# Where the first gate rows come from, where one modulation row is made, and where the last norms keep their tiles

## The chip, the cores and the metric

The kernel is one program on one core of a Trainium2 chip. Its time is the device time of one execution in microseconds (us). The profile is of one execution; its span runs from the first to the last instruction of the core. Engines are called PE (matmul), PEld (weight load), DVE, ACT, POOL and SP as in the profile; SP and POOL also issue DMAs, each on its own queue, in order.

## The reference, cut to what matters

One layer of a hybrid backbone on 512 latent tokens (and 256 context tokens) of width 1024. A token mixer (two families of gated scans, output projection, layer norm) comes first. The part that matters here is the second sublayer, a product-key expert retrieval over 128 x 128 single-neuron experts:

```python
q = (t @ w_query)...                      # 8 heads, two halves
s1, s2 = scores of the halves against 128 first keys and 128 second keys
v1, i1 = top_k(s1, 16); v2, i2 = top_k(s2, 16)
top_s, pos = top_k(all pair sums, 16)     # 16 experts per head, 128 per token
idx = first key * 128 + second key
g = softmax(top_s)
act = gelu(einsum('thkd,td->thk', expert_u[idx], t))
y   = einsum('thk,thkd->td', g * act, expert_v[idx])
x   = layer_norm(alpha * x + g2 * y) * gamma + beta      # the output
```

`g2` is one of six modulation rows, silu(c) times 1024 columns of `w_ada` plus a bias, the same for all tokens.

## The kernel before, in words

**Dense and fetched tokens.** Tokens are in four blocks of 128. For three blocks (`ND` = 3, `TD` = 384 tokens) the experts are computed densely: all 16,384 rows of `u` and `v` go through PE, and a gate matrix G[expert, token], zero where a token did not choose the expert, multiplies the activations. The fourth block (and the dot products with `u` of the last 16 tokens of the third) is fetched: POOL gathers, for one choice k at a time, one row of `u` or `v` for each of 128 tokens into a ring of six tiles `erow` (512 KB each, `fetched`, L1202 to L1249), and DVE multiplies and accumulates it (`dots` at L1235, `yg` at L1248).

**The gate matrix.** `gate_block` (L1115) makes it for 8 tokens at a time from one-hot matrices: DVE builds them, PE multiplies them into `pG`, ACT copies that to `stage`, a tile [128 second keys, 128 first keys, 32 tokens]. Each of the 12 stage tiles (2 MB) is stored to the DRAM tensor `Gd`. `gated` (L1165) reads it back, eight first keys and all 384 tokens at a time (`Gn`, 1.5 MB, two buffers), 16 times.

**Chunks.** There are 64 chunks of two first keys (256 experts). `hidden` (L1141) loads a chunk of `u` (`ur`, 1 MB), splits it into a high and a low part in `load_split` (`uh` by ACT at L1136, `ul` by DVE at L1137), makes 2 x 24 matmuls into `pH` and applies the activation into a `gel` tile. Part of `hidden` runs while the gate matrix is built (28 chunks are spilled to DRAM, `Hd`, and come back later); the rest runs in the main part, one beside each output chunk. An output chunk is `rows` (load `vr`, 1 MB, and split into `vh`, `vl`), `gated` (copy of 16 tokens' gates by ACT at L1177, product of `gel` and `Gn` by DVE at L1181, split into `ah` by ACT at L1186 and `al` by DVE at L1187) and `combine`: 2 x 18 matmuls `y` that accumulate in six PSUM banks over all chunks. The chunks' order is 0 to 3, 32 to 63, 4 to 31, and chunks 0 to 3 need the first eight first keys. The crossing is the place where the gate stage ends and the first `y` matmuls start. `vh` and `vl` have two buffers, one for each half of a chunk.

**The order of work.** A scheduler lays out each engine's instructions once, from the program and a cost model; an engine then runs them strictly in that order and waits at each for what it needs. POOL is in the program's order from the fourth block's picks on, ACT in the last three chunks.

**`g2`'s rows.** `mods_last` (L251) is a generator. After the last `hidden`, each further chunk advances it by one step: load 512 KB of `w_g2`, and multiply and sum what the step before loaded (L259). After eight steps `m2[:, 24:32]` holds the sums, and the bias is added (L264). `to_rows` (L266) turns that into rows: one PE transpose, one ACT copy (L272), one store to DRAM on POOL's queue (L273). `mod_row` (L275) loads the row as a broadcast on POOL's queue. Before, `to_rows` is called in the tail, just ahead of `mod_row`.

**The tail.** The last three chunks (`TAIL` = 3) are prepared, then multiplied block by block and half by half, so that `finish` (L1251), the residual sum and the layer norm of a block, can run while PE works on later blocks. `finish(3)`, the fetched block's, comes first and needs no PE; then `finish(0)`, `finish(1)`, `finish(2)`. `finish` has two tiles of 4 KB a partition, `x1` (loaded at L1256) and `r`; before, both are halves of a `vr` buffer of the later `v` ring. The row tiles g2, gamma and beta lie in a `Gn` buffer.

Of the kernel before, what the change touches and what calls it, by code (L numbers as in the profile page):

```python
# [8 lines left out]
F32 = mybir.dt.float32  # L9
F32R = mybir.dt.float32r  # L10
# [4 lines left out]
AF = mybir.ActivationFunctionType  # L15
# [4 lines left out]
D = 1024  # L20
# [11 lines left out]
class Net:  # L32
# [218 lines left out]
    def mods_last(self, pool):  # L251

        nc, a = self.nc, self.a
        sr = pool.tile([128, D], F32, name="silr")
        nc.sync.dma_start(sr, self.sild.to_broadcast([128, D]))
        m2 = self.m2[:, 24:32]
        for j in range(9):
            if j:
                nc.vector.scalar_tensor_tensor(w, w, 1.0, sr, op0=OP.mult, op1=OP.mult, accum_out=m2[:, j - 1:j])  # L259
            if j < 8:  # L260
                w = pool.tile([128, D], F32, name="wg2")
                nc.sync.dma_start(w, a["w_g2"][j])
                yield
        nc.vector.tensor_tensor(m2, m2, self.b2[:, 24:32], op=OP.add)  # L264

# [668 lines left out]
class Peer:  # L934
# [10 lines left out]
    GT = 32  # L945
# [169 lines left out]
    def gate_block(self, w, ps, b, kg):  # L1115

        nc, GT, GB = self.nc, self.GT, self.GB
        for q in range(128 // GT):
            stage = w.tile([128, 128, GT], F32, name="stage", bufs=2)
            for i in range(GT // GB):  # L1120
                self.gate_group(w, ps, kg, q * GT + i * GB, stage[:, :, i * GB:(i + 1) * GB])
                if i == GT // GB - 1:
                    nc.sync.dma_start(self.Gd[b * (128 // GT) + q], stage)
                yield
# [40 lines left out]
    def gated(self, n, pool, vpool, bufs, mark=None, home=None):  # L1165
# [4 lines left out]
        if 2 * n % self.GN == 0:  # L1170
            self.Gn = pool.tile([128, NG, self.GN, self.GT], F32, name="Gn", bufs=2)
            nc.sync.dma_start(self.Gn, self.Gd[:, :, 2 * n:2 * n + self.GN, :].rearrange("g m n t -> m g n t"))
# [9 lines left out]
        if home:  # L1182
            ah, al = (t.rearrange("p a b -> p (a b)")[:, 0:2 * self.TD].rearrange("p (e t) -> p e t", e=2) for t in home)
        else:
            ah, al = (vpool.tile([128, 2, self.TD], F32R, name=f"a{i}", bufs=bufs) for i in "hl")
# [65 lines left out]
    def finish(self, b, y, w, ring, rows, out):  # L1251
        nc = self.nc
        g2, gam, bet = rows
        two = ring.tile([128, 2, 8, 128], F32, name="vr", bufs=2)
        x1, r = (two[:, i].rearrange("p k c -> p (k c)") for i in range(2))
# [12 lines left out]
    def run(self, es, out):  # L1268
# [18 lines left out]
        with ExitStack() as e0:  # L1287
            gl = e0.enter_context(tc.tile_pool(name="gel", bufs=1, side="right", reuse_waits="tile"))
            up_es = e0.enter_context(ExitStack())
# [93 lines left out]
            with ExitStack() as e1:  # L1383
                w = e1.enter_context(tc.tile_pool(name="main", bufs=1, reuse_waits="tile"))
                yp = e1.enter_context(tc.tile_pool(name="yps", bufs=1, space=PSUM, reuse_waits="tile"))
# [5 lines left out]
                for i, m in enumerate(seq[:64 - self.TAIL]):  # L1391
# [12 lines left out]
                    elif i > first + 1:  # L1404
                        next(g2, None)
# [4 lines left out]
                    ops = self.gated(m, w, w, self.TAIL - 1, mark), v  # L1410
# [4 lines left out]
                for _ in g2:  # L1415
                    pass
# [4 lines left out]
                for c, m in enumerate(tail):  # L1421
# [6 lines left out]
                    acts.append(self.gated(m, w, w, self.TAIL - 1, mark, home and home[2]))  # L1428

                rows = w.tile([128, NG, self.GN, self.GT], F32, name="Gn", bufs=2)  # L1430
                rows = rows.rearrange("p g n t -> p (g n t)").rearrange("p (i d) -> p i d", i=3)
                n.to_rows(slice(24, 32), w, hps, "pH", n.q0[1][:, 0:128])
# [6 lines left out]
                self.finish(3, (yg[:, :512], yg[:, 512:]), bits, vp, rows, out)  # L1439
                for b in range(ND):  # L1440
# [4 lines left out]
                    self.finish(b, self.y[b], bits, vp, rows, out)  # L1445
# [32 lines left out]
```

## Time and profile before

| | |
|---|---|
| time before | 1745.32 us median of 3 runs (1743.29 to 1746.83) |
| the profiled execution | 1744.65 us, of which the span is 1742.7 us and 1.95 us lie around it |
| busy, share of the span | PE 95%, PEld 83%, DVE 83%, ACT 48%, POOL 28% |
| granted TensorE clock | 0.984 of full speed on average |
| DMA | 439.15 MB, 252 GB/s over the span |

A busy PE is modelled, so 95% is not PE at its peak. An engine's idle time counts only where it is what the end waits for; the view of the engines by stretches, the engines' timelines and the chain that ended last tell where that is. A timeline row gives the start, the busy time, the engine, the line, the operation with its output and inputs, how many instructions were merged into the row, and in brackets how long the engine sat idle before it and what ended that.

### The profile page before, as it was taken

The page shows a single profiled execution, that of the slowest core. Times are in us where ns is not written, and L with a number is a line of the kernel's source. Part 1 is how long each engine was busy: PE and PEld are TensorE (multiplying, and loading weights), DVE is VectorE, ACT ScalarE, POOL GpSimd, SP SyncE. Part 2 cuts the span into 40 slices and gives each one's busy share as a digit, 9 for nine tenths or more (in the row PEclk, how much of TensorE's full clock was granted, in tenths as well). Part 3 has the DMA queues.
Part 4 walks back from the last instruction along what each step waited for, and adds up shares of the span by engine and source line. Part 5 has one row for each costly group of instructions (what it writes and reads, how often), then busy time and mean ns, then how long its engine had stood idle before and what let it go on. Part 6 is the DMA issues. An engine that isn't in the chain of part 4 may idle for free. (4 is left out here: it accounts for less than half of the span.)

```text
span 1742.7 us, 27586 instructions
## 1 busy us (share of the span) xinstructions
PE 1657.3 (95%) x10440; PEld 1450.2 (83%) x10440; DVE 1455.1 (83%) x2888; ACT 833.2 (48%) x1413; POOL 486.9 (28%) x323
## 2 busy tenths in 40 slices
PE   6999999989999999999996999999999999999995
PEld 3888877877788999999996899999999998778884
DVE  6689888877989999999995887787787777778777
ACT  4667677655233364777663333333333333233331
POOL 0000000000043002232573554454555453234300
PEclk9999999989999999999998999999999999999998
DMA  9345345134322247889889989989989989999962
GB/s 330 117 146 164 129 145 179 58 144 153 145 87 72 98 156 273 296 331 339 327 320 399 357 307 340 348 303 339 350 306 342 341 287 368 364 321 354 340 210 97
DMA packets 128999, 439.15 MB, mean 252 GB/s; under 512 B 12465, under 2 KB 44625, under 8 KB 109922
## 3 DMA queue, kind: packets, MB, share of 16 engines
q1 hardware_dynamic: 88018, 289.94, 47.1%
q0 software_dynamic: 40272, 145.36, 22.9%
q8 instruction: 81, 1.33, 0.3%
q10 hardware_dynamic: 576, 2.10, 0.3%
q14 instruction: 52, 0.43, 0.1%
HBM read 388.95 MB, written 48.40 MB: 251 GB/s over the span
## 5 line engine op out<-in xcount | busy, mean ns | idle before, releaser
L141 PE MATMUL pH<-hh,ul 128*128 128x368 f32 x1024 | 339.0, 332 | 4.1 <-DVE ul L1137 4.1
L139 PE MATMUL pH<-hh,uh 128*128 128x368 f32 x1024 | 339.4, 331 | 1.8 <-ACT gels L1155 1.8
L140 PE MATMUL pH<-hl,uh 128*128 128x368 f32 x1024 | 337.0, 329 | 0.0
L139 PE MATMUL y<-vh,ah 128*128 128x512 f32 x756 | 297.2, 393 | 16.6 <-ACT ah L1186 16.5
L140 PE MATMUL y<-vl,ah 128*128 128x512 f32 x756 | 296.5, 392 | 2.3 <-DVE vl L1137 2.3
L141 PE MATMUL y<-vh,al 128*128 128x512 f32 x756 | 295.6, 392 | 1.4 <-DVE al L1187 1.4
L1219 POOL DMA_INDIRECT erow<-in_v_dram,ix x128 | 214.0, 1672 | 268.6 <-DVE yg L1248 142.4
L1219 POOL DMA_INDIRECT erow<-in_u_dram,ix x128 | 206.8, 1616 | 228.5 <-DVE erow L1235 127.1
L1137 DVE TENSOR_TENSOR vl<-vr,vh 128x1024 fp32r<-128x1024 f32 x126 | 153.7, 1222 | 111.6 <-ACT vh L1136 111.4
L1136 ACT ACTIVATE uh<-ur 128x1024 fp32r<-128x1024 f32 x128 | 135.6, 1060 | 218.7 <-PE pH L140 197.3
L1136 ACT ACTIVATE vh<-vr 128x1024 fp32r<-128x1024 f32 x126 | 131.9, 1055 | 169.0 <-PE y L141 134.0
L141 PEld LDWEIGHTS pH<-hh,ul 128*128 128x128 f32 x1024 | 192.0, 188 | 5.8 <-DVE ul L1137 5.8
L139 PEld LDWEIGHTS pH<-hh,uh 128*128 128x128 f32 x1024 | 192.3, 188 | 3.5 <-ACT gels L1155 2.3
L140 PEld LDWEIGHTS pH<-hl,uh 128*128 128x128 f32 x1024 | 192.2, 188 | 1.2
L139 PEld LDWEIGHTS y<-vh,ah 128*128 128x128 f32 x756 | 143.1, 189 | 47.6 <-ACT ah L1186 18.9
L141 PEld LDWEIGHTS y<-vh,al 128*128 128x128 f32 x756 | 143.1, 189 | 32.8 <-DVE al L1187 2.7
L140 PEld LDWEIGHTS y<-vl,ah 128*128 128x128 f32 x756 | 143.2, 189 | 31.3 <-DVE vl L1137 2.7
L1235 DVE SCALAR_TENSOR_TENSOR erow<-erow,h 128x1024 f32<-128x1024 f32 x128 | 151.8, 1220 | 15.7 <-DMA erow<-in_u_dram,ix 15.7
L1248 DVE SCALAR_TENSOR_TENSOR yg<-erow,q,yg 128x1024 f32<-128x1024 f32 x127 | 162.9, 1283 | 0.1
L1137 DVE TENSOR_TENSOR ul<-ur,uh 128x1024 fp32r<-128x1024 f32 x128 | 154.8, 1220 | 9.7 <-ACT uh L1136 9.6
L139 PE MATMUL pc<-hTh,wh 128*128 128x512 f32 (+1 forms) x304 | 109.6, 361 | 0.3 <-ACT G L381 0.3
L140 PE MATMUL pc<-hTl,wh 128*128 128x512 f32 (+1 forms) x304 | 108.1, 356 | 0.0
(408 smaller groups left out, 3045.0 us busy)
## 6 DMA issues: line engine op xcount, KB each, us to landing
ur<-in_uT_dram SPq DMA_DIRECT2D x64, 1024.0 KB, 7.8
vr<-in_vd_dram SPq DMA_DIRECT2D x64, 1024.0 KB, 6.7
Gd<-stage SPq DMA_DIRECT2D x12, 2048.0 KB, 10.0
Gn<-Gd SPq DMA_DIRECT2D x16, 1536.0 KB, 13.0
wraw<-in_w_cf_dram SPq DMA_DIRECT2D x24, 512.0 KB, 4.0
wada<-in_w_ada_dram SPq DMA_DIRECT2D x48, 256.0 KB, 3.0
Hd<-gels SPq DMA_DIRECT2D x28, 368.0 KB, 5.2
gel<-Hd SPq DMA_DIRECT2D x28, 368.0 KB, 6.0
```

The lines of the kernel that those rows point to most:

```text
L139: mm(out, lh, rh, start=start, stop=False)
L140: mm(out, lh, rl, start=False, stop=False)
L141: mm(out, ll, rh, start=False, stop=stop)
L1136: nc.scalar.activation(hi, raw[:, e], AF.Copy)
L1137: self.mark = nc.vector.tensor_tensor(lo, raw[:, e], hi, op=OP.subtract).ins
L1219: nc.gpsimd.indirect_dma_start(out=e, out_offset=None, in_=a["v" if src == "v" else "u"], in_offset=bass.IndirectOffsetOnAxis(ap=ix[:, j:j ...
L1235: nc.vector.scalar_tensor_tensor(e, e, 1.0, h2, op0=OP.mult, op1=OP.mult, accum_out=dots[:, j:j + 1])
L1248: nc.vector.scalar_tensor_tensor(y, e, act[:, j:j + 1], y, op0=OP.mult, op1=OP.add)
```

## The change

1. **First gates on chip.** When a stage tile is full, ACT copies its first eight first keys into a `Gn` tile that stays on chip (12 copies of 128 x 256), and the store to `Gd` leaves these keys out (1.875 MB in place of 2 MB). `gated` doesn't load `Gn` for chunk 0. The two `Gn` buffers now come from two pools, one opened ahead of the `u` ring and one in the main part, and `new_gates` takes them in turn. `gated` takes its `ah` and `al` tiles ahead of the load.
2. **`g2`'s rows in the main part.** `mods_last` yields True after the bias is added, and the main loop then calls `to_rows`. The tail only calls `mod_row`.
3. **Last norms in the fetched rows' ring.** `finish` takes `x1` and `r` as two tiles of the `erow` ring.

```diff
@@ -260,8 +260,9 @@
             if j < 8:
                 w = pool.tile([128, D], F32, name="wg2")
                 nc.sync.dma_start(w, a["w_g2"][j])
-                yield
+                yield False
         nc.vector.tensor_tensor(m2, m2, self.b2[:, 24:32], op=OP.add)
+        yield True
 
     def to_rows(self, js, pool, ps, tag, row=None):
 
@@ -1120,7 +1121,9 @@
             for i in range(GT // GB):
                 self.gate_group(w, ps, kg, q * GT + i * GB, stage[:, :, i * GB:(i + 1) * GB])
                 if i == GT // GB - 1:
-                    nc.sync.dma_start(self.Gd[b * (128 // GT) + q], stage)
+                    at = b * (128 // GT) + q
+                    nc.scalar.activation(self.Gn[:, at], stage[:, 0:self.GN, :], AF.Copy)
+                    nc.sync.dma_start(self.Gd[at, :, self.GN:, :], stage[:, self.GN:, :])
                 yield
 
 
@@ -1162,13 +1165,23 @@
             r = self.gel[n] = ring.tile([128, 2, self.TD], F32, name="gel", bufs=self.AHEAD + 1)
             self.nc.sync.dma_start(r[:, :, :self.TU], self.Hd[n - self.AHEAD])
 
-    def gated(self, n, pool, vpool, bufs, mark=None, home=None):
+    def new_gates(self):
+
+        self.gates.append(self.gates.pop(0))
+        self.Gn = self.gates[-1].tile([128, self.TD // self.GT, self.GN, self.GT], F32, name="Gn")
+        return self.Gn
+
+    def gated(self, n, vpool, bufs, mark=None, home=None):
 
         nc = self.nc
         NG, NU = self.TD // self.GT, self.TU // self.GT
         rest = self.TU % self.GT
-        if 2 * n % self.GN == 0:
-            self.Gn = pool.tile([128, NG, self.GN, self.GT], F32, name="Gn", bufs=2)
+        if home:
+            ah, al = (t.rearrange("p a b -> p (a b)")[:, 0:2 * self.TD].rearrange("p (e t) -> p e t", e=2) for t in home)
+        else:
+            ah, al = (vpool.tile([128, 2, self.TD], F32R, name=f"a{i}", bufs=bufs) for i in "hl")
+        if 2 * n % self.GN == 0 and n:
+            self.new_gates()
             nc.sync.dma_start(self.Gn, self.Gd[:, :, 2 * n:2 * n + self.GN, :].rearrange("g m n t -> m g n t"))
         g = self.gel.pop(n)
         g4 = g.rearrange("p n (g t) -> p n g t", t=self.GT)
@@ -1179,10 +1192,6 @@
             for t in [(slice(0, NU),)] + [(NU, slice(0, rest))] * (rest > 0):
                 at = (slice(None), slice(None), *t)
                 nc.vector.tensor_tensor(g4[at], g4[at], gates[at], op=OP.mult)
-        if home:
-            ah, al = (t.rearrange("p a b -> p (a b)")[:, 0:2 * self.TD].rearrange("p (e t) -> p e t", e=2) for t in home)
-        else:
-            ah, al = (vpool.tile([128, 2, self.TD], F32R, name=f"a{i}", bufs=bufs) for i in "hl")
         nc.scalar.activation(ah, g, AF.Copy)
         nc.vector.tensor_tensor(al, g, ah, op=OP.subtract)
         return ah, al
@@ -1251,8 +1260,7 @@
     def finish(self, b, y, w, ring, rows, out):
         nc = self.nc
         g2, gam, bet = rows
-        two = ring.tile([128, 2, 8, 128], F32, name="vr", bufs=2)
-        x1, r = (two[:, i].rearrange("p k c -> p (k c)") for i in range(2))
+        x1, r = (ring.tile([128, D], F32, name="erow", bufs=self.LOOK + 1) for _ in range(2))
         nc.sync.dma_start(x1, self.n.x1d[b])
         halves = [slice(hf * 512, (hf + 1) * 512) for hf in range(2)]
         st = w.tile([128, 12], F32, name="stz").rearrange("p (h s) -> p h s", h=2)
@@ -1286,6 +1294,8 @@
         yg = n.yg
         with ExitStack() as e0:
             gl = e0.enter_context(tc.tile_pool(name="gel", bufs=1, side="right", reuse_waits="tile"))
+            self.gates = [e0.enter_context(tc.tile_pool(name="gates", bufs=1, side="right", reuse_waits="tile"))]
+            self.new_gates()
             up_es = e0.enter_context(ExitStack())
             up = up_es.enter_context(tc.tile_pool(name="uring", bufs=1, side="right", reuse_waits="tile"))
             nh, asked = 0, 0.0
@@ -1382,6 +1392,7 @@
                             more(first + (out_to - first) * at / groups - asked)
             with ExitStack() as e1:
                 w = e1.enter_context(tc.tile_pool(name="main", bufs=1, reuse_waits="tile"))
+                self.gates.insert(0, w)
                 yp = e1.enter_context(tc.tile_pool(name="yps", bufs=1, space=PSUM, reuse_waits="tile"))
                 self.y = [tuple(yp.tile([128, 512], F32, name=f"y{b}{hf}") for hf in range(2)) for b in range(ND)]
                 ahead = self.AHEAD - 1
@@ -1402,18 +1413,17 @@
                             first = i
                             g2 = n.mods_last(vp)
                     elif i > first + 1:
-                        next(g2, None)
+                        if next(g2, False):
+                            n.to_rows(slice(24, 32), w, hps, "pH", n.q0[1][:, 0:128])
                     fetch(rate)
                     v = self.rows(m, vp if vp and i > first + 1 and (i - first) % 2 == 0 else w)
                     if nh == 64 and i + ahead < 64:
                         self.back(seq[i + ahead], gl)
-                    ops = self.gated(m, w, w, self.TAIL - 1, mark), v
+                    ops = self.gated(m, w, self.TAIL - 1, mark), v
                     for e in range(2):
                         for b in range(ND):
                             self.combine(2 * m, e, b, ops)
                 fetch(256)
-                for _ in g2:
-                    pass
                 manual.close()
                 e1.enter_context(tc.manual_schedule(engines={mybir.EngineType.Activation}))
                 tail = seq[64 - self.TAIL:]
@@ -1425,24 +1435,23 @@
                         [t[:, 2 * j:2 * j + 2, :].rearrange("p a (b c) -> p (a b) c", c=128) for t in (self.hh, self.hl)]
                         for j in range(3)]
                     vs.append(self.rows(m, (vp, w)[(64 - self.TAIL + c - first) % 2], home and home[:2]))
-                    acts.append(self.gated(m, w, w, self.TAIL - 1, mark, home and home[2]))
-
-                rows = w.tile([128, NG, self.GN, self.GT], F32, name="Gn", bufs=2)
+                    acts.append(self.gated(m, w, self.TAIL - 1, mark, home and home[2]))
+
+                rows = self.new_gates()
                 rows = rows.rearrange("p g n t -> p (g n t)").rearrange("p (i d) -> p i d", i=3)
-                n.to_rows(slice(24, 32), w, hps, "pH", n.q0[1][:, 0:128])
                 n.mod_row(rows[:, 0], 3)
                 nc.sync.dma_start(rows[:, 1], a["ln_g"][1:2].to_broadcast([128, D]))
                 nc.sync.dma_start(rows[:, 2], a["ln_b"][1:2].to_broadcast([128, D]))
                 nc.scalar.preload_act_table_set("natural_log_exp_and_others")
                 rows = [rows[:, i] for i in range(3)]
                 bits = Bits(n.q0[1][:, 128:])
-                self.finish(3, (yg[:, :512], yg[:, 512:]), bits, vp, rows, out)
+                self.finish(3, (yg[:, :512], yg[:, 512:]), bits, fp, rows, out)
                 for b in range(ND):
                     for hf in range(2):
                         for i, a_, v in zip(tail, acts, vs):
                             for e in range(2):
                                 self.combine(2 * i, e, b, (a_, v), (hf,))
-                    self.finish(b, self.y[b], bits, vp, rows, out)
+                    self.finish(b, self.y[b], bits, fp, rows, out)
 
 
 def build(tc, a, out):
```

## Rows read from the trace of the kernel before

**Rows 1.** Stretches: us, busy of PE, PEld, DVE, ACT, POOL, clock, DMA share, GB/s.

```profile
740.00:760.00 20.00, 19.80 (x164) 19.22 (x163) 20.00 (x32) 14.30 (x32) 5.16 (x4) 1.00 0.96 359
...
925.00:930.00 5.00, 5.00 (x32) 5.00 (x31) 0.00 (x0) 0.48 (x1) 0.00 (x0) 1.00 1.03 428
...
935.00:940.00 5.00, 0.00 (x0) 0.00 (x0) 3.49 (x5) 2.95 (x3) 1.66 (x2) 0.72 1.07 363
...
945.00:950.00 5.00, 3.38 (x8) 2.71 (x9) 5.00 (x9) 2.54 (x4) 3.66 (x3) 0.50 1.02 416
...
1530.00:1540.00 10.00, 10.00 (x46) 8.29 (x45) 10.00 (x13) 4.47 (x7) 5.78 (x3) 1.00 0.83 285
```

**Rows 2.** Timeline of PE at the crossing, 926 to 972 us.

```profile
934.38 0.33 PE L141 MATMUL pH<-hh,ul 128*128 128x368 f32 x1
...
946.62 0.80 PE L139 MATMUL y<-vh,ah 128*128 128x512 f32 x1 [11.91 <-ACT ah L1186]
...
959.55 0.50 PE L140 MATMUL y<-vl,ah 128*128 128x512 f32 x1 [2.28 <-DVE vl L1137]
```

**Rows 3.** Timeline of ACT at the crossing.

```profile
935.97 2.00 ACT L1136 ACTIVATE vh<-vr 128x1024 fp32r<-128x1024 f32 x2 [2.71 <-DMA vr<-in_vd_dram]
...
943.45 0.59 ACT L1177 ACTIVATE gel<-Gn 128x32 f32<-128x32 f32 x4 [4.54 <-DMA Gn<-Gd]
...
945.72 0.84 ACT L1186 ACTIVATE ah<-gel 128x768 fp32r<-128x768 f32 x1 [1.68 <-DVE gel L1181]
```

**Rows 4.** Timeline of DVE at the crossing.

```profile
923.67 1.23 DVE L1137 TENSOR_TENSOR ul<-ur,uh 128x1024 fp32r<-128x1024 f32 x1 [2.77 <-ACT uh L1136]
...
940.08 2.35 DVE L1137 TENSOR_TENSOR vl<-vr,vh 128x1024 fp32r<-128x1024 f32 x2
...
957.13 1.23 DVE L1235 SCALAR_TENSOR_TENSOR erow<-erow,h 128x1024 f32<-128x1024 f32 x1 [2.55 <-DMA erow<-in_u_dram,ix]
...
958.28 1.22 DVE L1137 TENSOR_TENSOR vl<-vr,vh 128x1024 fp32r<-128x1024 f32 x1
```

**Rows 5.** Timeline of SP's queue at the crossing.

```profile
912.66 0.32 SPq L1123 DMA_DIRECT2D Gd<-stage  x1
...
921.21 0.51 SPq L1132 DMA_DIRECT2D vr<-in_vd_dram  x1
...
926.27 0.38 SPq L1172 DMA_DIRECT2D Gn<-Gd  x1
```

**Rows 6.** ACT by line and shape while gates are built, 690 to 915 us.

```profile
L1102 ACT ACTIVATE ohg<-oh,g2f 128x128 bf16<-128x128 bf16 x192 | 65.5, 436 | 10.2 <-DVE oh L1095 7.5 <-DVE g2f L1082 2.7
...
L1113 ACT ACTIVATE stage<-pG 128x512 f32<-128x512 f32 x96 | 53.6, 596 | 13.9 <-PE pG L1112 13.1
```

**Rows 7.** Timeline of DVE in the tail.

```profile
1706.86 0.96 DVE L1187 TENSOR_TENSOR hl<-gel,hh 128x768 fp32r<-128x768 f32 x1 [0.96 <-ACT hh L1186]
...
1713.66 1.29 DVE L1260 TENSOR_TENSOR vr<-yg,Gn 128x512 f32<-128x512 f32 x2 [5.84 <-DMA Gn<-m2d]
...
1738.19 1.41 DVE L135 SCALAR_TENSOR_TENSOR vr<-vr,q,Gn 128x512 f32<-128x512 f32 x2
```

**Rows 8.** Timeline of POOL's queue, at 1529 us and in the tail.

```profile
1528.87 1.69 POOL L1219 DMA_INDIRECT erow<-in_u_dram,ix  x1 [8.58 <-DVE yg L1248]
...
1707.27 0.57 POOL L273 DMA_DIRECT2D m2d<-q  x1 [41.97 <-ACT q L272]
...
1709.49 0.58 POOL L278 DMA_DIRECT2D Gn<-m2d  x1 [1.65 <-PE y L141]
```

**Rows 9.** Timeline of PE, its last matmul.

```profile
1724.18 0.39 PE L141 MATMUL y<-hh,hl 128*128 128x512 f32 x1
```

**Rows 10.** DVE by line in the tail: the last norms' operations.

```profile
L134 DVE SCALAR_TENSOR_TENSOR vr<-vr,q,Gn 128x512 f32<-128x512 f32 x8 | 5.6, 746 | 0.1
...
L1261 DVE SCALAR_TENSOR_TENSOR vr<-vr 128x512 f32<-128x512 f32 x8 | 5.1, 683 | 0.0
...
L1260 DVE TENSOR_TENSOR vr<-y,Gn 128x512 f32<-128x512 f32 x6 | 3.9, 664 | 0.0
```

## The prediction

> **What bounds the kernel now.** I read the stretches first. Through the main part PE is full; the stretch at 1530 us stands for it [rows 1], with 46 matmuls in 10 us, so 0.22 us for one `y` matmul. What the change touches counts only where PE or the end waits, and that is in two places.
>
> The first is the crossing. The last `pH` matmul starts at 934.38 and takes 0.33 us, the first `y` matmul starts at 946.62 after 11.91 us of idleness, which ended with `ah` [rows 2]. Going back along ACT: `ah` at 945.72 waited for DVE's product, that for ACT's copy of the gates at 943.45, and that for `Gn` from `Gd` [rows 3]. On SP's queue the `Gn` load was issued at 926.27, behind the last `Gd` store (912.66) and the first `vr` load (921.21) [rows 5]; so 17.2 us passed until its data could be used. Others were late as well: `vr` was there only at 935.97 [rows 3], and `vl` came only at 940.08 [rows 4]. The DMA engines were at their full share throughout, 363 to 428 GB/s [rows 1]. A second, short wait follows: PE idles 2.28 us before 959.55 for the next chunk's `vl` [rows 2], which DVE did at 958.28, behind a product that had waited 2.55 us for a gathered row [rows 4].
>
> The second place is the tail. The chain that ended last is all DVE. DVE's timeline shows why: `al` of the last chunk ends at 1706.86 + 0.96 = 1707.82, then DVE idles 5.84 us until g2's row lands, starts `finish(3)` at 1713.66, and is dense until 1738.19 + 1.41 = 1739.60 [rows 7]. The row was late because its store was issued at 1707.27 after ACT's copy, and its broadcast at 1709.49 [rows 8]. PE ended at 1724.18 + 0.39 = 1724.57 [rows 9], 15.0 us before DVE.
>
> **Part 1, gates on chip.** It adds 12 ACT copies of 128 x 256. The trace has none of that shape; the nearest are 128 x 512 out of PSUM at 596 ns and 128 x 128 at 436 ns [rows 6], and 128 x 32 at 0.59 us for four, with overlap [rows 3]. So 0.15 to 0.60 us each, and I take 0.44, which makes 12 x 0.44 = 5.3 us of ACT (1.8 to 7.2). They lie beside DVE, which is full in that stage while ACT is busy 14.30 of 20 us [rows 1]. I cost them at nothing; uncovered, they would cost all 5.3 us. The Trainium skill, page "ScalarE: Activation LUTs", section "What ACT_TABLE_LOAD costs", gives 186 ns and 0.833 ns an element for an ACTIVATE with immediate operands, hence 0.40 us and 4.8 us in all as an estimate; exposed, the sum would be 1739 instead of 1734. No run here shows this shape yet.
>
> It removes 12 x 128 KB of stores and one load of 1.5 MB. All but the last store lie in the stage that DVE bounds, so they are worth nothing. The load and the last store's share lie in the crossing: 1.57 + 0.13 = 1.70 MB, at the 416 GB/s of its last stretch [rows 1] 4.1 us. What does that buy PE? If the load had no successors, nothing: below, the second wait decides, for if the gathered row of 957.13 lands when it did, `vl` comes at 958.28 again and everything before it was only rearranged, a gain of 0. From above, `vr` still comes at 935.97, ahead of the removed load in the same queue; with `vh` (half of 2.00 us) and `vl` (half of 2.35) behind it `y` can't flow before 938.2, so the first hole shrinks by at most 8.4 us, and with the 2.28 us the gain is at most 10.7. In DVE's present order `vl` at 940.08 would let `y` flow at 941.3, 5.3 us earlier. But what comes after, gathered rows and the next chunks' loads, waits for DMA engines that are full, and these get free 4.1 us earlier. I take 4 us, since the share of 1.02 to 1.07 [rows 1] says that bytes decide here.
>
> The Trainium skill, page "DMA: Bandwidth & Descriptors", section "Issuing engines are not separate DMA queues", says that DMAs run on the same 16 DMA engines and interleave whichever engine issued them. By it what SP no longer moves helps POOL's gathers too, but by no more than its bytes: it speaks for the 4 and against the 10.7. The trace agrees as far as the share at 1.00 shows it.
>
> The clock: right after the hole PE ran at 0.50, the lower of its two levels (1.2 of 2.4 GHz), 8 matmuls in 3.38 us [rows 1], 0.42 each. A hole of 8 us would still be followed by some of that, so I take no gain from it.
>
> The order in which ACT and DVE take new work may change. `ah` and `al` of chunk 0 can now be made while DVE is idle (0.00 of 5 us from 925 [rows 1]); that empties DVE's queue a little later on, which I count within the 4.
>
> **Part 2, g2's rows.** One transpose, one ACT copy, one store leave the tail and stand behind the bias at about 1531. PE and ACT pay what they paid. POOL is in program order, so its store waits there for ACT, and the gathers behind it wait too. There POOL idled 8.58 us before 1528.87 [rows 8] and PE stayed full from 1530 on [rows 1]; a hold of that length is covered by the five rows that are asked for ahead. I cost it at nothing; longer, each microsecond is one of PE's. In the tail POOL has had nothing to do since 1665 (1707.27 - 41.97), so the broadcast can go out as soon as a `Gn` buffer is free, and DVE's 5.84 us go.
>
> **Part 3, the ring.** Four buffers' worth of `x1` and `r` in six tiles: the loads of `x1` no longer wait for the last `v` chunk. By itself that is worth nothing, since DVE was dense after 1713.66; but together with part 2 it lets `finish(3)` start before 1707.82, in DVE's gaps, where the schedule puts it. What follows on DVE: 25.94 us for four blocks from 1713.66, 6.49 each [rows 7]. Starting at 1707.82 DVE ends 5.84 us earlier; this is the lower bound. From above PE bounds it: after 1724.57 the last half block needs L1260, L1261 and the statistics (0.66, 0.68 and about as much again), and two each of L134 and, alike, L135 at 0.75 [rows 10], together 5.0 us, so no end before 1729.6, a gain of at most 10.0. I take 7, the lower bound and the 0.96 us gap right ahead of `al` [rows 7], rounded: the gaps that I can name on DVE's row are nearer to the lower end.
>
> **Sum.** 1744.65 - 4 (crossing) - 7 (tail) - 0 (copies, transposition) = 1733.65. The runs' median stands 0.67 above the profiled execution, so 1734.3, and I say **1734**.
>
> **The rivals.**
> - *The gathers decide the crossing.* The rows land as before and PE waits again for `vl` near 958. For it: rows 4's 2.55 us. Against: the shared engines' full share. Only the tail gains: 1745.3 - 7 = 1738.3.
> - *Both ends go to their bounds.* `y` flows before 939 and `finish(3)` vanishes in DVE's gaps: 1745.3 - 10.7 - 10.0 = 1724.6. For it: DVE's idle stretch at 925 [rows 1]. Against: DMA bytes.
> - *The tail change doesn't do what it says.* `finish(3)` still starts near 1713 because something else is late, `x1` behind the last gathered rows or the broadcast behind POOL's queue. Only the crossing gains: 1741.3. Against: POOL had been idle 41.97 us before 1707.27 [rows 8].
> - *Slower: PE's order at the crossing.* With gates at hand the schedule may put the first `y` matmuls ahead of the 48 `pH` matmuls that now fill PE up to 934.71. At the 32 in 5 us of [rows 1], 7.5 us of cover are lost: PE would wait from 927.2 for `vr`. If `y` still starts at 946.62, that costs 7.5 us, against 5.84 from the tail: 1747. It decides (over 0.2% slower) once `y` starts later than 948.5, for example because `ah`, whose tiles are now taken ahead of the load, lands on space that the last store at 912.66 still reads: 1749. Against: `pH` is ready first.
>
> **How the numbers follow.** 0.2%, 3.5 us, is about what a measurement of this kernel tells from no change. Forecast 0.39; gathers decide 0.22; both bounds 0.17; tail not delivered 0.10, half of it within 0.2%; copies exposed or a milder form of the last rival, about 1744, 0.04; slower 0.08. Faster is 0.39 + 0.22 + 0.17 + 0.05 = 0.83, same 0.09, slower 0.08. The range from 1724 to 1742 leaves out part of the bounds' case (0.05), the last two (0.12) and a little of the tail's case, under 0.2 in all. The forecast's own range is 1730 to 1737.
>
> **What would show it.** Crossing: no `Gn` load before the first `y`; the hole on PE at 934 ends by about 941, with ACT's first copy of gates long before; the second wait is what to look at: if it grows by what the first lost, the gathers decide. Tail: `m2d` stored near 1531, its broadcast before 1700, no DVE idleness between `al` and `finish(3)`, DVE's end 5 to 8 us after PE's instead of 15. Gate stage: 12 new ACT rows of 0.4 us and DVE still full. Wrong would be: PE idle from 927, POOL held long at 1531 with PE idle behind it, or a `finish(3)` that waits for `x1`.

## The result and the profile after

The changed kernel takes 1736.57 us (median of 5 runs, 1734.64 to 1738.59), the kernel before 1746.83 in the same rounds (1743.29 to 1748.76). The ratio is 0.9946, with a 95% interval of 0.9931 to 0.9961: about 9.4 us less, from 6.8 to 12. The forecast was 1734 in a range of 1724 to 1742. The profiled execution of the changed kernel took 1737.73 us, of which its span is 1736.0; it started its first `pH` matmul 4.5 us later than the profiled execution of before (488.5 against 484.0), with the same instructions ahead of it, so stages are compared here from their own beginning and not by the clock on the wall.

**The crossing.** The timelines of PE, ACT, DVE and SP's queue of the changed kernel there, in this order (start, us, engine and line, and in brackets the idle time ahead and what ended it):

```profile
937.62 0.44 PE L139 MATMUL pH<-hh,uh 128*128 128x368 f32 x1 [1.93 <-ACT gel L1158]
940.96 2.50 PE L139 MATMUL y<-vh,ah 128*128 128x512 f32 x5 [2.90 <-ACT vh L1139]
947.63 0.79 PE L140 MATMUL y<-vl,ah 128*128 128x512 f32 x1 [4.17 <-DVE vl L1140]
```

```profile
917.67 0.42 ACT L1125 ACTIVATE Gn<-stage 128x256 f32<-128x256 f32 x1
918.12 0.59 ACT L1190 ACTIVATE gel<-Gn 128x32 f32<-128x32 f32 x4
...
930.18 0.85 ACT L1195 ACTIVATE ah<-gel 128x768 fp32r<-128x768 f32 x1 [5.51 <-DMA Gd<-stage]
...
939.85 2.00 ACT L1139 ACTIVATE vh<-vr 128x1024 fp32r<-128x1024 f32 x2 [2.29 <-DMA vr<-in_vd_dram]
```

```profile
936.51 1.23 DVE L1244 SCALAR_TENSOR_TENSOR erow<-erow,h 128x1024 f32<-128x1024 f32 x1 [2.91 <-DMA erow<-in_u_dram,ix]
...
940.29 1.22 DVE L1244 SCALAR_TENSOR_TENSOR erow<-erow,h 128x1024 f32<-128x1024 f32 x1 [2.55 <-DMA erow<-in_u_dram,ix]
...
944.07 1.23 DVE L1244 SCALAR_TENSOR_TENSOR erow<-erow,h 128x1024 f32<-128x1024 f32 x1 [2.55 <-DMA erow<-in_u_dram,ix]
...
946.36 2.35 DVE L1140 TENSOR_TENSOR vl<-vr,vh 128x1024 fp32r<-128x1024 f32 x2
```

```profile
917.67 0.32 SPq L1126 DMA_DIRECT2D Gd<-stage  x1
...
925.89 1.04 SPq L1135 DMA_DIRECT2D vr<-in_vd_dram  x2
933.63 0.33 SPq L1135 DMA_DIRECT2D ur<-in_uT_dram  x1
...
949.16 0.39 SPq L1185 DMA_DIRECT2D Gn<-Gd  x1
```

SP's queue of the kernel before, behind the rows of [rows 5]:

```profile
942.84 7.23 SPq L1132 DMA_DIRECT2D ur<-in_uT_dram  x2
```

Follow them back from PE. The one hole of 11.91 us [rows 2] has become three shorter ones, and the second wait at 959.55 [rows 2] is gone. The gates are in place at 918.7, while in the kernel before they were copied out at 943.45 [rows 3]; no `Gn` load stands ahead of the first `y`. `ah` was nevertheless made only at 930.18, because its tile lies on the staging buffer that the last `Gd` store reads. What `y` waits for is first `vr`, then `vl`, and `vl` stands on DVE behind three dots, each of which waited for a gathered row. The first 5 `y` matmuls ran on `vh` alone; `y` flows from 947.63. The room that the `Gn` load left in SP's queue went to the next `ur` load (1 MB), which is issued at 933.63, ahead of the first `y`; in the kernel before that came at 942.84.

**The second part and the tail.** First POOL's queue, then PE where it has a hole that the kernel before does not have, then DVE and PE at the end, all of the changed kernel:

```profile
1517.96 1.69 POOL L1228 DMA_INDIRECT erow<-in_u_dram,ix  x1 [2.94 <-DVE yg L1257]
1536.82 0.56 POOL L274 DMA_DIRECT2D m2d<-q  x1 [17.17 <-ACT q L273]
1537.68 1.91 POOL L1228 DMA_INDIRECT erow<-in_u_dram,ix  x1 [0.30 <-DVE al L1196]
...
1679.88 0.57 POOL L279 DMA_DIRECT2D Gn<-m2d  x1 [14.93 <-DVE gel L1194]
```

```profile
1560.69 0.50 PE L139 MATMUL y<-vh,ah 128*128 128x512 f32 x1 [2.31 <-ACT ah L1195]
1561.68 0.80 PE L141 MATMUL y<-vh,al 128*128 128x512 f32 x1 [0.26 <-DVE al L1196]
```

```profile
1689.38 1.29 DVE L1268 TENSOR_TENSOR erow<-yg,Gn 128x512 f32<-128x512 f32 x2 [2.36 <-DMA Gn<-m2d]
...
1709.07 0.96 DVE L1196 TENSOR_TENSOR hl<-gel,hh 128x768 fp32r<-128x768 f32 x1 [0.96 <-ACT hh L1195]
1710.91 1.41 DVE L135 SCALAR_TENSOR_TENSOR erow<-erow,q,Gn 128x512 f32<-128x512 f32 x2 [0.89 <-ACT q L128]
...
1731.38 1.41 DVE L135 SCALAR_TENSOR_TENSOR erow<-erow,q,Gn 128x512 f32<-128x512 f32 x2
```

```profile
1726.17 0.39 PE L141 MATMUL y<-hh,hl 128*128 128x512 f32 x1
```

The store of g2's row held POOL for 17.17 us. Its broadcast went out at 1679.88, not 1709.49 [rows 8], and `finish(3)` started at 1689.38, not 1713.66 [rows 7]; only its last line comes after the last `al`. DVE ends at 1731.38 + 1.41 = 1732.79, 6.2 us after PE's last matmul (1726.17 + 0.39) instead of 15.0.

Single executions of this kernel differ by some 5 us, so the experiments below are read by three sums from their traces, beside the ratios. **Crossing**: the gaps of over 0.5 us between starts of successive matmuls from 918 us to the 289th `y`, each less the usual 0.23; shorter gaps are left out. **Second part**: the same from the last `pH` to the last `y`. **Tail**: from the start of the last `y` to the end of the last instruction in DVE's queue, which comes some 3 us after DVE's last norm. The table has them in us, with the milestone that the expectations speak of. Between crossing and second part PE took 370.7 us in each of the 14 kernels, so nothing is won or lost there.

| kernel | last `pG` to 289th `y` | crossing | second part | tail | median of its runs, us | ratio, 95% interval |
|---|---|---|---|---|---|---|
| before | 163.5 | 14.8 | 7.0 | 18.5 | | |
| changed | 157.7 | 10.4 | 10.7 | 9.7 | 1736.57 | 0.9946 (0.9931 to 0.9961) |
| gates_only | 159.3 | 12.2 | 5.0 | 18.4 | 1739.99 | 0.9983 (0.9968 to 0.9997) |
| rows_only | 161.4 | 13.9 | 8.8 | 9.3 | 1739.97 | 0.9979 (0.9964 to 0.9994) |
| ring_only | 165.5 | 16.5 | 5.5 | 18.1 | 1742.99 | 1.0002 (0.9984 to 1.0020) |
| late_rows | 158.9 | 11.6 | 6.5 | 12.5 | 1736.47 | 0.9946 (0.9923 to 0.9969) |
| early_load | 154.8 | 6.1 | 10.3 | 9.4 | 1732.90 | 0.9940 (0.9926 to 0.9954) |
| pad_acts | 163.8 | 14.8 | 11.1 | 9.4 | 1734.49 | 0.9955 (0.9941 to 0.9969) |
| hold_gathers | 145.7 | 0.0 | 15.7 | 10.7 | 1731.59 | 0.9930 (0.9913 to 0.9946) |
| act_store | 157.3 | 8.9 | 7.0 | 9.6 | 1729.90 | 0.9924 (0.9907 to 0.9941) |
| hold_even | 146.9 | 0.3 | 9.3 | 9.5 | 1725.56 | 0.9900 (0.9878 to 0.9923) |
| hold_even_act | 146.6 | 1.1 | 8.1 | 9.8 | 1724.51 | 0.9895 (0.9862 to 0.9929) |
| vl_first | 157.7 | 9.5 | 12.2 | 9.4 | 1735.25 | 0.9944 (0.9926 to 0.9962) |
| hold_early | 147.3 | 1.9 | 10.2 | 9.9 | 1724.17 | 0.9893 (0.9862 to 0.9924) |

The four lines after "changed" ran in one group, the next four in a second, the last four in a third; the kernel before had medians of 1744.03, 1742.94 and 1743.23 us there, and each ratio is to its own group.

### The profile page after: what moved, and what is told of

Its sections match the earlier page's. It is cut to its first block, busy times and chain, and to the rows that moved or that the text cites. A ratio compares the mean times of both kernels' runs of the same rounds, so it can differ in the third digit from the quotient of the medians.

```text
span 1736.0 us, 27602 instructions
## 1 busy us (share of the span) xinstructions
PE 1662.7 (96%) x10440; PEld 1453.7 (84%) x10440; DVE 1455.3 (84%) x2888; ACT 836.3 (48%) x1425; POOL 482.9 (28%) x323
## 4 chain that ended last, share of the span: by engine, by line
PE 57%; DVE 27%; DMA 8%; issue 5%; ACT 3%; POOL 0%; SPq 0%; DVEq 0%; ACTq 0%; POOLq 0%
PE y L141 7%; PE y L140 7%; PE pH L141 7%; PE y L139 7%; PE pH L139 7%; PE pH L140 7%; DVE ul L1140 2%; PE pG L1113 2%; PE pc L141 2%; PE pc L139 2%; PE pc L140 2%; DMA Gn<-Gd 2%; DVE ohg L1101 2%; DVE oh L1096 1%; DMA wada<-in_w_ada_dram 1%
```

## Experiments: which part does what

**gates_only**: part 1 alone; g2's rows and the ring of the last norms as before.

> The kernel before with part 1 alone (first gates copied on chip, their store and load left out). My theory, that the crossing gives some 5 us: 1742 us beside 1746.8 (0.997), the last pG matmul to the 289th y matmul takes about 158 us instead of 163.5, and the tail is as before (DVE ends 15 us after PE, with a wait of 5 to 6 us for g2's row). The rival, that the tail gave all of the change's gain: 1746 to 1747, with the crossing's stretch still near 163.

Measured: 0.9983. The crossing has 12.2 us of holes, the tail 18.4 as before. Part 1 is worth about 3 us by the ratio (0.5 to 5.6).

**rows_only**: part 2 alone, on the kernel before.

```diff
-                        next(g2, None)
+                        if next(g2, False):
+                            n.to_rows(slice(24, 32), w, hps, "pH", n.q0[1][:, 0:128])
...
-                n.to_rows(slice(24, 32), w, hps, "pH", n.q0[1][:, 0:128])
                 n.mod_row(rows[:, 0], 3)
```

> The kernel before with part 2 alone (g2's rows made in the main part; norms still in the v ring). My theory: the tail needs the early row only, x1 being there in time from the v ring, so DVE ends 7 to 9 us after PE instead of 15; and POOL is held some 17 us near 1520 to 1540, which costs PE about 4 us near 1560: net 1743 us (0.998). The rival, that without the ring the first norm waits for x1 instead: DVE ends 12 to 15 us after PE, time 1746 to 1750.

Measured: 0.9979, tail 9.3, POOL held 17.06 us, and the same hole of PE that the changed kernel has:

```profile
1536.52 0.56 POOL L274 DMA_DIRECT2D m2d<-q  x1 [17.06 <-ACT q L273]
```

```profile
1559.82 0.50 PE L139 MATMUL y<-vh,ah 128*128 128x512 f32 x1 [1.74 <-ACT ah L1187]
```

(POOL's timeline, then PE's.) The tail's whole gain, 9.2 us, comes without the ring of part 3, and part of it is given back: the second part has 8.8 us of holes, where kernels without the hold have 5.0 to 7.0, and the ratio leaves 3.7 us.

**ring_only**: part 3 alone, on the kernel before: `x1` and `r` in `erow` tiles of the ring `fetch`.

> The kernel before with part 3 alone (last norms' tiles in the fetched rows' ring). My theory: nothing, 1746 to 1748 (1.000), because the first norm still waits for g2's row after 1707 and DVE is dense from there. The rival, that the loads of x1 bounded the tail: 2 to 4 us faster.

Measured: 1.0002, tail 18.1. Part 3 alone does nothing, as expected. The three parts' ratios multiply to 0.9964, beside 0.9946 for the whole; the intervals leave room for that.

**late_rows**: the changed kernel with the row made behind the last gather.

```diff
-                        if next(g2, False):
-                            n.to_rows(slice(24, 32), w, hps, "pH", n.q0[1][:, 0:128])
+                        next(g2, None)
                 fetch(256)
+                n.to_rows(slice(24, 32), w, hps, "pH", n.q0[1][:, 0:128])
```

> The changed kernel with g2's rows made after the last gather has been asked for, not in the middle of the gathers, so that POOL's store holds no gather. My theory, that the hold cost PE about 4 us near 1560: no hold at 1520 to 1540, no PE gap at 1558, 1732 to 1734 us (0.992 of before), the tail as in the changed kernel. The rival, that the gap at 1558 has another cause (the Gn load alone): the gap stays and the time is the changed kernel's, 1736 to 1738.

Measured: 0.9946. The hold and its hole are gone (second part 6.5), but the tail was expected as in the changed kernel and is 12.5: POOL's queue was free, but the row's copy was not there. The ratio was expected at 0.992, so this is a miss.

```profile
1703.38 0.57 POOL L274 DMA_DIRECT2D m2d<-q  x1 [35.78 <-ACT gel L1190]
1705.51 0.57 POOL L279 DMA_DIRECT2D Gn<-m2d  x1 [1.56 <-DVE al L1196]
```

PE and ACT run in order too: the transpose (L271) was laid at 1701.67 and the copy (L273) at 1702.83, among the last chunks' work, though the sums were ready at 1531. So of the 4.2 us that this wins in the second part, 2.8 are lost in the tail.

**act_store**: the changed kernel with the row's store issued by ACT, right behind its own copy. PE, DVE and SP keep their order.

```diff
-        nc.gpsimd.dma_start(self.m2d[0, js, :], r)
+        (by or nc.gpsimd).dma_start(self.m2d[0, js, :], r)
...
-    n.to_rows(slice(24, 32), w, hps, "pH", n.q0[1][:, 0:128])
+    n.to_rows(slice(24, 32), w, hps, "pH", n.q0[1][:, 0:128], nc.scalar)
```

> The changed kernel with the one store of g2's row issued by ACT, right behind its own copy, instead of by POOL; all else stands in the same order on every engine. Theory: POOL is not held for 17 us at 1520 to 1537, the gathers keep their even pace, PE has no gap of 2 to 3 us near 1558, the time from the last pH to the last y is 277 to 278 us instead of 281 to 283, and the tail stays 9 to 10 us: 1732 to 1734, ratio 0.993. Rival: the hold is covered by the rows asked for ahead and the gap at 1558 has another cause (the Gn load then); the gap stays and the time is that of the changed kernel, 1736.6.

Measured: 0.9924 against 0.9946 of the changed kernel, with intervals that overlap by 0.001; second part 7.0 as in the kernel before, tail 9.6. The stretch from the last `pH` to the last `y` fell only from 282.6 to 280.7, not to the expected 277 to 278; this execution has 22 gaps of 0.3 to 0.5 us there, which the sum of holes leaves out, and the changed kernel 15. The stretches of the second part (us, busy PE, PEld, DVE, ACT, POOL, clock, DMA share, GB/s), first of the changed kernel, then of act_store:

```profile
1540.00:1550.00 10.00, 10.00 (x46) 8.29 (x45) 8.91 (x12) 2.86 (x3) 8.19 (x6) 1.00 0.97 333
1550.00:1570.00 20.00, 17.43 (x69) 13.68 (x69) 9.25 (x13) 5.76 (x9) 4.92 (x3) 0.91 0.92 322
```

```profile
1540.00:1550.00 10.00, 10.00 (x46) 8.29 (x45) 8.45 (x12) 3.88 (x4) 4.01 (x3) 1.00 0.96 331
1550.00:1570.00 20.00, 20.00 (x90) 16.57 (x89) 15.06 (x23) 6.62 (x11) 8.77 (x6) 1.00 0.98 339
```

In 20 us PE starts 90 matmuls instead of 69: 21 x 0.23 = 4.8 us lost in the changed kernel here, 2.57 as idleness and the rest at a lower clock (0.91 on the mean). The chain is this: held for 17 us, POOL then issues its gathers one after another (six busy issues in the first stretch instead of three), they share the DMA engines with SP's `Gn` load, issued at 1543.20, and ACT gets that load only at 1559.67, 16.5 us later. In act_store the same load was issued at 1544.03 and used at 1554.67, 10.6 us later:

```profile
1554.67 0.23 ACT L1190 ACTIVATE gel<-Gn 128x32 f32<-128x32 f32 x1 [4.63 <-DMA Gn<-Gd]
```

```profile
1559.67 0.23 ACT L1190 ACTIVATE gel<-Gn 128x32 f32<-128x32 f32 x1 [12.43 <-DMA Gn<-Gd]
```

(ACT's timeline, act_store, then the changed kernel.) So the hold does not cost what stands behind it in POOL's queue; it costs what the bunched gathers delay in SP's.

## Experiments: what the crossing waits for

**early_load**: the changed kernel with 1.5 MB of gates loaded where the kernel before had its first `Gn` load, for chunk 32, whose own load, at 949.16 in the changed kernel, then falls away.

```diff
-        if 2 * n % self.GN == 0 and n:
+        k = 64 if n == 0 else 2 * n
+        if k % self.GN == 0 and n != 32:
...
+            if n == 0:
+                self.early, self.Gn = self.Gn, now
+        if n == 32:
+            self.Gn = self.early
```

> The changed kernel, with a 1.5 MB load put back between the first vr load and the next two: it fetches the gates of keys 64 to 71 for chunk 32, where the kernel before fetched those of keys 0 to 7. The bytes are back, the dependence of ah on them is not; the later load for chunk 32 is gone. Milestone: from the last pG matmul to the 289th y matmul, 157.7 us in the changed kernel, 163.5 in the kernel before. If the bytes are what the crossing pays for, it goes back to 161 to 163 and the time to 1741 or so. If the dependence (copy of gates, product, ah, all behind the load) is, it stays at 157 to 159 and the time at that of the changed kernel (1736.6, ratio 0.995). I hold it for bytes at two to one, since the engines' share was 1.0 in both.

Measured: 0.9940, a milestone of 154.8, and 6.1 us of holes, where the changed kernel has 10.4. SP's queue, then PE:

```profile
929.40 0.42 SPq L1135 DMA_DIRECT2D vr<-in_vd_dram  x1
931.34 0.38 SPq L1187 DMA_DIRECT2D Gn<-Gd  x1
931.78 16.87 SPq L1135 DMA_DIRECT2D vr<-in_vd_dram  x2
948.70 0.42 SPq L1135 DMA_DIRECT2D ur<-in_uT_dram  x1
```

```profile
947.21 0.80 PE L140 MATMUL y<-vl,ah 128*128 128x512 f32 x1 [1.28 <-DVE vl L1140]
```

My preferred theory falls: the load at that place costs nothing that shows. Up to here the queue has the order of the kernel before (`vr`, `Gn`, two `vr`, `ur`), and 6.1 us of holes stand against 14.8. What paid is then the dependence of `ah` on the load. Two limits: the scheduler put the 1 MB `ur` load, which the changed kernel issues at 933.63, behind `Gn`, and the load of 949.16 is gone, so the transfers are reordered and not more; what 1.5 MB on top would cost was not tried. And the third dot waited only 0.80 us for its row (2.55 in the changed kernel), so part of the 4.3 us between 6.1 and 10.4 belongs to this execution. The two ratios' intervals still allow a loss of up to some 2.5 us.

**pad_acts**: a 4 KB tile taken ahead of `ah`, so that it does not lie on the staging buffer.

> The changed kernel with 4 KB a partition left free ahead of ah and al, so that the first ah no longer lies on the staging buffer that the last store of gates reads (in the changed kernel it waited 5.5 us for that store, until 930.18). Theory: y waits for vr and vl, not for ah, so that ah at 925 instead of 930 gives 0 to 1 us: milestone 157 to 159, ratio as the changed kernel, 0.995. Rival: DVE then makes al and the next products in its idle time from 925 and y flows up to 3 us earlier: 154 to 155.

Measured: 0.9955, no gain. The trace does not isolate the question: a late gather held DVE for 10.56 us until 922.47, and `ah`, which waited 11.13 us for DVE's product, came at 929.37. That `ah`'s place costs nothing rests on the timeline of the changed kernel, where `y` waits for `vh` and `vl` long after `ah`.

**hold_gathers**: the changed kernel without the gathers beside the first chunk.

```diff
-                    rate = self.ROWS[1] if nh < 64 else self.ROWS[2]
+                    rate = 0 if i == 0 else self.ROWS[1] if nh < 64 else self.ROWS[2]
```

> The changed kernel without the gathers that are asked for beside the main part's first chunk; the same rows are gathered in later chunks or after the last of the first 61. Theory: in the changed kernel the two vl of chunk 0 stand on DVE behind three dots, each of which waited 2.5 to 2.9 us for a row (936.51, 940.29, 944.07); with those gone vl comes with vr at about 941, y flows at 942 to 943 without the 4.2 us wait before 947.63, and the milestone from the last pG to the 289th y goes from 157.7 to 152 to 154. The rows have to be fetched later, so the whole may gain less: 1732 to 1736. Rival: the engines' bytes gate vr and not the dots; then vl comes no earlier and the milestone stays within 156 to 159.

Measured: the crossing has no hole at all; `y` starts at 934.0. 10 us are won, more than expected (milestone 145.7, expected 152 to 154), and the rows that are then missing cost 5 of them in the second part, where PE waits: 0.9930.

**hold_even**: the same, with the missing 5.4 rows spread over the next 31 chunks.

```diff
-                    rate = self.ROWS[1] if nh < 64 else self.ROWS[2]
+                    rate = (self.ROWS[1] * 32 / 31 if i else 0) if nh < 64 else self.ROWS[2]
```

> The changed kernel, nothing gathered beside the main part's first chunk, and the 5.4 rows that are missing spread evenly over the next 31 chunks (2.787 instead of 2.7 a step), so that the second part starts with as many rows done as in the changed kernel. When the same rows were left to the end, the milestone from the last pG to the 289th y fell from 157.7 to 145.7, and the stretch from the last pH to the last y grew from 282.6 to 290.9. Theory: the gathers were what the crossing still paid for, and the engines have room in the steady part (share 0.9), so here the milestone is 145 to 149 and the later stretch again 280 to 284: 1724 to 1728, ratio 0.988 to 0.991. Rival: the steady part has no room for more rows, PE waits there, and last y comes as late as before: 1731 to 1736.

Measured: 0.9900, crossing 0.3, second part 9.3. The steady part takes the rows for nothing. ACT, then PE:

```profile
940.01 2.01 ACT L1139 ACTIVATE vh<-vr 128x1024 fp32r<-128x1024 f32 x2 [0.97 <-DMA vr<-in_vd_dram]
```

```profile
941.12 1.43 PE L139 MATMUL y<-vh,ah 128*128 128x512 f32 x5 [0.19 <-ACT vh L1139]
```

The first chunk's `vr` load was issued at 930.55, the next chunk's right behind it, so `vr` took 9.5 us; with the gathers beside it 14.0 (925.89 to 939.85). In the other kernels it is 9.0 to 9.2 without gathers beside it and 13.0 to 14.8 with them, but for pad_acts (11.0). And `vl` follows `vh` by 1.1 us (941.10), behind the waiting dots by 6.5 (946.36). Both add up to the 10 us: 4.5 with the gathers off the DMA engines, 5.4 with the dots out of DVE's way.

**hold_even_act**: hold_even and act_store together.

> The same, and the store of g2's row issued by ACT: if the two add, the stretch after the last pH is 277 to 281, no gap of PE over 1 us near 1540 to 1550, tail 9 to 10.5, and the time 1721 to 1725, ratio 0.986 to 0.989. Rival: with denser gathers the tail's or the second part's loads decide, and nothing comes on top of the spread gathers alone.

Measured: 0.9895, 1724.51 us, at the upper end of the expected time. By the ratio the addition is not told apart from hold_even, as the intervals overlap; by the trace the hole near 1550 is gone and the second part is 8.1 instead of 9.3. It beats both kernels.

**vl_first**: the first chunk's gathers asked for behind its `vl`, the same number of rows.

```diff
-                    fetch(rate)
+                    if i:
+                        fetch(rate)
...
                     ops = self.gated(m, w, self.TAIL - 1, mark), v
+                    if i == 0:
+                        fetch(2 * rate)
```

> The changed kernel, with the first chunk's gathers asked for behind its vl and ah instead of ahead: the same number of rows by the end of the chunk, but on DVE the dots stand behind vl. If DVE's order is what holds y (vl behind three dots), y flows as soon as vh is there, and the milestone goes to 146 to 152, with a second wait at the next chunk's vl at most 2 us; time 1728 to 1733. If the bytes of the gathers hold vr itself, vr comes at 940 as in the changed kernel, vl at 942, and the milestone is 153 to 156.

Measured: 0.9944, a miss. `y` starts at 930.6, but then stops for 8.16 us: on DVE the dots now stand ahead of the next chunk's `vl` (951.25) and product (953.52), and one of them waited 4.16 us for its row, until 944.17:

```profile
930.57 1.47 PE L139 MATMUL y<-vh,ah 128*128 128x512 f32 x5 [0.34 <-ACT vh L1139]
...
955.43 0.80 PE L139 MATMUL y<-vh,ah 128*128 128x512 f32 x1 [8.16 <-ACT ah L1195]
```

At this place within the crossing the gathers cost as much as before; taking them out of it gains.

**hold_early**: hold_even with the load of early_load.

> The kernel with the gathers spread, and the 1.5 MB load of gates put back at the crossing (keys 64 to 71, for a later chunk, so that nothing of this chunk waits for it). With the gathers there, the same load cost nothing that showed (ratio 0.994 as without it). If that was because the load hid behind the gathers, it now costs its bytes: vh 3 to 4 us later, milestone 149 to 153 against that of the kernel with spread gathers alone, ratio 0.002 more. If the first chunk's y doesn't need what the load delays, no difference: both within 0.001.

Measured: 0.9893 against 0.9900, 1.9 us of holes against 0.3. The load costs next to nothing here either; that it hid behind the gathers is not borne out, though intervals of 0.003 can't exclude a ratio 0.002 larger. The first chunk's `vr` is issued ahead of it, only the next two stand behind it in SP's queue, and `vh` of the first chunk still came 9.2 us after its issue (924.15 to 933.37). As in early_load, `ur` moved behind the load and the later load is gone.

## Why the prediction was right, and where it was not

**Part 1, the crossing: 4 us, for a reason that the runs do not bear out.** Without the change the crossing has 14.8, 13.9 and 16.5 us of holes (before, rows_only, ring_only), with it 10.4, 12.2, 11.6 and 8.9 (changed, gates_only, late_rows, act_store): 4.3 less on the mean, and 3.0 (0.5 to 5.6) by the ratio of gates_only. Single executions spread by some 2 us about these means. The prediction argued that "bytes decide here", 1.70 MB at 416 GB/s. early_load has the kernel before's order of loads up to the first `y` and less than half its holes, and in the changed kernel a `ur` load took the freed room. What went is the chain load, copy, product, `ah`. The prediction described it, found 5.3 us for it ("would let `y` flow at 941.3") and set that aside for the bytes, whose 4.1 lies so near to what was measured that the number does not tell the two apart. In the three kernels without the change `ah` ends the wait, 5.4 us after `vl` is there; in those with it, `vl` does. What stayed is the wait for gathered rows. The rival "the gathers decide the crossing" was half right: `y` did wait for `vl` behind the dots until 947.63, yet the wait at 959.55 vanished, where that rival had it grow. The change stayed within its bounds of 0 and 10.7. hold_even shows that 14.5 us of holes can go, more than that upper bound, because `vr` itself, which the bound held fixed, comes earlier without the gathers.

The rule that the prediction cited, the Trainium skill, page "DMA: Bandwidth & Descriptors", section "Issuing engines are not separate DMA queues", holds in these traces: SP's `vr` load took 14.0 us beside POOL's gathers and 9.5 without. What did not follow from it is that freed bytes become time.

**Copies at nothing: right.** The view by line of ACT while gates are built:

```profile
L1125 ACT ACTIVATE Gn<-stage 128x256 f32<-128x256 f32 x12 | 5.0, 417 | 0.2
```

417 ns against an estimate of 440, and the time from the first `pH` to the last `pG` is 426.6 us, against 426.5 before. The Trainium skill's page "ScalarE: Activation LUTs", section "What ACT_TABLE_LOAD costs", gave 0.40 us as an estimate; the trace agrees.

**`ah` on the last store's space: it happened, and cost nothing here.** The prediction named it within the slower rival. `ah` waited 5.51 us for that store, but `vr` came 9 us later still. The order of `pH` ahead of `y` stayed.

**Part 2 at nothing: the step that failed.** The prediction took a hold of 8.58 us and five rows asked for ahead as its cover. The hold was 17.17 us: POOL came to the store at 1519.65, 9.5 us before DVE added the bias (1529.14), and then the transpose stood in PE's order until 1533.58 and the copy in ACT's until 1536.28. The second part has 10.7, 8.8, 10.3 and 11.1 us of holes with it (changed, rows_only, early_load, pad_acts) against 7.0, 5.0, 5.5 and 6.5 without (before, gates_only, ring_only, late_rows): 4.2 us. The prediction's own price for a longer hold, each microsecond one of PE's, would have made 8.6. The cover named held for the rows themselves: by the waits of DVE from 1518 to 1600 us, no dot and no `yg` waited for one. The price came from the bunch of gathers afterwards, which the prediction did not follow, though it named POOL held long with PE idle behind it as a sign of being wrong. act_store, which differs in that store's queue alone, shows it: 3.7 us less of holes, 0.9924 against 0.9946.

**The tail: 7 forecast, 8.8 measured** (18.5 to 9.7), within its bounds of 5.84 and 10.0. `finish(3)` went into DVE's gaps for all but its last line, so the value nearer to the bound that PE sets would have been the better choice. The rival of a tail that is not delivered had no part in it.

**Part 3: "together with part 2 it lets `finish(3)` start before 1707.82"** is wrong: in rows_only `finish(3)` starts at 1696.43 and the tail is 9.3, without the ring.

**The sum.** -4.3 + 4.2 - 8.8 = -8.9 us, against -9.4 by the ratio. The forecast had -4 + 0 - 7 = -11.

## What to carry to other kernels

Before a DMA is moved in a queue that runs in order, ask for how long it will wait there, and then what the held requests do when they come all at once: here the bunch delayed another queue's load by 6 us, and PE by 4. Where an engine waits behind full DMA engines, look at which single transfer its chain needs; here the place of a 1.5 MB load made no difference that shows, the dependence on it was worth 3 to 4 us, and moving some five gathers out of the crossing into a stretch where PE hides them another 8 (0.9946 to 0.9900). An operation that waits for data, placed ahead of work that is ready on the same engine, makes that work late as well: the dots ahead of `vl` cost about as much as the shared transfers (5.4 and 4.5 us).

## What was not expected of the hardware

In 6 of the 14 profiles, none of them the two main ones, one gather was in issue on POOL for 24 to 32 us between 858 and 913 (act_store, early_load, gates_only, hold_even, late_rows, pad_acts), where others there took 0.9 to 8.2. From early_load, POOL's timeline, DVE's, then the stretches (columns as above):

```profile
867.06 3.23 POOL L1234 DMA_INDIRECT erow<-in_v_dram,ix  x1 [0.64 <-DVE yg L1263]
870.93 32.08 POOL L1234 DMA_INDIRECT erow<-in_v_dram,ix  x1 [0.64 <-DVE yg L1263]
903.32 0.95 POOL L1234 DMA_INDIRECT erow<-in_v_dram,ix  x1 [0.30 <-issue]
```

```profile
900.97 1.21 DVE L1096 TENSOR_TENSOR oh<-iota,kT 128x2048 bf16<-128x2048 bf16 x1
909.05 1.28 DVE L1263 SCALAR_TENSOR_TENSOR yg<-erow,q,yg 128x1024 f32<-128x1024 f32 x1 [6.86 <-DMA erow<-in_v_dram,ix]
```

```profile
870.00:903.00 33.00, 33.00 (x320) 31.83 (x319) 32.19 (x40) 24.71 (x56) 32.36 (x2) 1.00 0.65 239
905.00:910.00 5.00, 2.61 (x16) 2.30 (x14) 0.95 (x1) 0.29 (x1) 3.36 (x4) 1.00 1.00 394
```

DVE was busy for 32.19 of the 33 us. It fell idle at 902.18, waiting for a gathered row, and the issue ended 0.8 us later, at 903.01; PE then waited too (busy 2.61 of 5 us). In all six profiles the issue ended 0.8 us after DVE had fallen idle. pad_acts' late row of 922.47 follows such an issue, which ended at 912.73. In five of the six the time from the first `pH` to the last `pG` was 3 to 7 us longer than the 426.5 us of before, in pad_acts 2 shorter; in the profiles without it, it was 1 us shorter to 2.3 longer. That is as much as single executions differ. The rows suggest that DVE's work held up the issue; no run tried it, so the cause stays open.
